# Row maxima of a windowed attention: spread over the partitions through DRAM in GpSimd's queue instead of by TensorE transposes, exponentials one quarter later

## The chip, the cores and the metric

The kernel runs on one core of a Trainium2 chip. The metric is the time of one execution on the device, in microseconds (us), as the median of repeated runs. The times of the kernel before are 628.92, 630.24 and 630.98 us (median 630.24).

## The reference

One layer of a diffusion backbone, in float32, on 1024 latent tokens of width 1024 (a grid of 16 rows by 64 columns) and 256 context tokens. Cut to what matters here:

```python
h  = rmsnorm(x, norm_g) * (1 + scale) + shift          # adaLN from c
q, k, v, za, u, bg, cg, zc = split(h @ w_in)           # eight blocks of 512 columns
q, k = rmsnorm per head of 64                          # 8 heads
s_lat = rope(q) . rope(k) * scale + bias               # each query sees an 8 x 16 window
s_ctx = q . kc * scale                                 # and all 256 context keys
p = softmax(concat(s_lat, s_ctx))                      # one softmax over both
o = p_lat @ v + p_ctx @ vc
attn = o * silu(za)
conv = bg * conv3(cg * u) * silu(zc)
out = x + gate * (concat(attn, conv) @ w_out)
```

The softmax needs, for every query, a maximum over its keys. The kernel holds scores with keys on the partitions and queries along the free dimension, so that maximum runs across partitions, and the result has to stand on all 128 partitions to be subtracted.

## The kernel before, in words

**Stages.** Up to about 60 us the kernel loads and transposes x and multiplies the first columns; from there to about 273 us it projects q, k, v for the eight heads and spills them to DRAM; from about 274 to 512 us it runs the attention; then it ends the convolution and multiplies by `w_out`. Float32 products are split into high and low float32r parts, three TensorE matmuls for each product (`mm3`).

**The attention stage** is a loop over quarters (`quarter(n)`): a head has four quarters of 256 queries, so there are 32 with scores and a few more at the end that drain the pipeline. TensorE's idle places are filled with projection work for the gates and the convolution: the generator `fill`, one step of which (a *tick*) is six matmuls of 512 columns into the tile `pu`. The table `TICKS` says how many ticks each quarter gets; its length is the number of quarters.

**One quarter** issues on TensorE the latent scores (tile `pss`), the context scores of the next quarter (`pc`), the transposes of row maxima (`pmx`), ticks, and the products with v of an earlier quarter (tile `po`: `lat_out` for the window, `ctx_out` for the context keys of two quarters at once, in every second quarter and at its very start; such a quarter is called early in the code). VectorE adds the bias (`sb<-pss,bt`), takes maxima (`mx<-pc,sc`, `mx<-mx,sb`), subtracts them (`sc<-sc,mg`, `sb<-sb,mg`) and makes the low parts (`plc`, `pll`) of what ScalarE exponentiated (`phc`, `phl`).

**The maxima** (`maxima(e)`, L1135 on). `mx` holds for each partition and query the maximum over the keys of that partition. TensorE transposes up to two blocks of 128 queries of it (`pmx<-ci,mx`), VectorE reduces along the free dimension to `rm` (queries on the partitions, one column for each block). The inner function `back` then transposes a broadcast of `rm` on TensorE (`pmx<-ci,rm`), which puts each maximum on all partitions, and ScalarE copies it from PSUM to `mg`. `back` is called between the matmuls of `ctx_out` or `ctx_scores`, so that TensorE has other work while VectorE reduces.

**Order.** In this stage every instruction of TensorE, ScalarE and VectorE, and GpSimd's computing instructions, are chained in the order in which the code issues them. The DMAs of SyncE and GpSimd are not; the scheduler places them in their queues, and a queue then runs in order. Quarter n exponentiates the scores of quarter `e = n - 2` and multiplies with v those of `o = n - 3`.

Of the kernel before, what the change touches and what calls it, by code (L numbers as in the profile page):

```python
# [10 lines left out]
F32 = mybir.dt.float32  # L11
# [8 lines left out]
P = 128  # L20
# [6 lines left out]
NH, HD = 8, 64  # L27
# [2 lines left out]
CTXT = 3  # L30
FORDER = [4, 5, 6, 0, 1, 2, 3, 7]

TICKS = [2, 3, 3, 3, 3, 2, 3, 3, 2] + 2 * (8 * [3] + 2 * [4]) + 3 * [3] + [5, 4, 4]
EPS = 1e-6


# [3 lines left out]
def body(tc, es, x, ctxt, w_ada, b_ada, w_in, q_g, k_g, rpbr, w_out, vecs, cst, out):  # L40
    nc = tc.nc
# [20 lines left out]
    pe, act, dve, pool = every = [ordered(e) for e in (nc.tensor, nc.scalar, nc.vector, nc.gpsimd)]  # L62
# [27 lines left out]
    def many(name, n, shape):  # L90
        return [dr.tile(shape, F32, name=f"{name}{i}")[:] for i in range(n)]
# [14 lines left out]
    v_d = many("v_d", NPAIR, [P, 2, 2, NB + 2, HD + 1])  # L106
    kc_d = many("kc_d", NPAIR, [P, 2, L])
    ri_d = many("ri_d", NPAIR, [2, T])


    cp = es.enter_context(sbuf("cp"))
    ci = cp.tile([P, P + 2], F32, name="ci")
    ident = ci[:, 0:P]
# [213 lines left out]
    def do_frees(most):  # L327
        while most > 0 and slow and slow[0][2] is not None and not slow[0][0]:
            slow.pop(0)[1]()
            most -= 1  # L330
        return most
# [508 lines left out]
    for m in range(1, 4):  # L840
        k, new, last = 2 * m, m < 3, m == 3
# [169 lines left out]
    class head:  # L1011
# [31 lines left out]
        def ctx_scores(self, g, between=None):  # L1043
            pc = psm.tile([P, 2, 256], F32, name="pc", tag="C", bufs=2)
            q = self.q[:, 1, g * 256:(g + 1) * 256]
            for i in range(2):
                if i and between:
                    between()
                for l in range(2):
                    pe.matmul(pc[:, i], self.kc[:, l, i * P:(i + 1) * P], q,  # L1050
                              start=(i == 0 and l == 0), stop=(i == 1 and l == 1), skip_group_check=True)
            sc = ap.tile([P, 2, 256], F32, name="sc", tag="sc", bufs=4)
            act.copy(sc, pc)
            self.cps[g] = sc, pc

# [58 lines left out]
    def pair_of(n):  # L1114

        h, g = divmod(n, 4)
        return [(a, heads[h], 2 * g + a) for a in range(2)] if 0 <= h < NH else []
# [12 lines left out]
    def turned(n):  # L1130

        g = n % 4
        return [b for b, there in (((2 * g + 2) % NB, n + 1 < 4 * NH), (2 * g + 1, n >= 0)) if there][::-1 if g < 3 else 1]

    def maxima(e):  # L1135

        blocks = turned(e) if e < 4 * NH else []
        nb = len(blocks)
        if not blocks:
            return None  # L1140
        pm = psm.tile([P, 512], F32, name="pmx", tag="C", bufs=2)
        for i, b in enumerate(blocks):
            pe.transpose(pm[:, i * P:(i + 1) * P], mx[:, b * P:(b + 1) * P], ident)
        rm = ap.tile([P, 2], F32, name="rm", tag="rm", bufs=8)
        dve.tensor_reduce(rm[:, :nb], pm[:, :nb * P].rearrange("p (i k) -> p i k", i=nb), AX.X, ALU.max)

        def back():
            for i in range(nb):
                pe.transpose(pm[:, 256 + i * P:256 + (i + 1) * P], rm[:, i:i + 1].broadcast_to([P, P]), ident)
            v, step = mg[:, blocks[0] * P:], (blocks[-1] - blocks[0]) * P or P  # L1150
            act.copy(bass.AP(v.tensor, v.offset, [list(v.ap)[0], [step, nb], [1, P]]),
                     pm[:, 256:256 + nb * P].rearrange("p (i k) -> p i k", i=nb))
        return back

    def quarter(n):

        live = lambda m: 0 <= m < 4 * NH  # L1160
        ticks = TICKS[n]
        e, o = n - 2, n - 3
        left = do_frees(1) + 2 if n > 2 else 3
        back = maxima(e) if e >= 0 else None
        while lat_rest:
            lat_rest.pop()()
        early = live(o) and o % 2
        if early:
            heads[o // 4].ctx_out(o % 4, back)
        do_dves(left)  # L1170
        if gating and next(gating[0], "end"):
            gating.pop(0)
        now = pair_of(n)
        for i, hd_, j in now:
            hd_.scores(j, sbank[:, i])
        if n == 0:
            next(fill)
            ticks -= 1
        ctx_now = [m for m in ([0, 1] if n == 0 else [n + 1]) if live(m)]
        for m in ctx_now:  # L1180
            heads[m // 4].ctx_scores(m % 4, back if n >= 2 and not early else None)
        if back and not early and not ctx_now:
            if not now:
                next(fill, None)
                ticks -= 1
            back()
        def biased():
            sb = sbs[n] = sb_new()
            bt = now[0][1].bt[:].rearrange("p v n -> p (v n)")[:, :1128].rearrange("p (a n) -> p a n", a=2)
            for at, slot, w_ in (((0, 31, 8), (8, 15, 16)), ((0, 0, 31),), ((0, 0, 31),), ((0, 0, 15), (15, 39, 8)))[n % 4]:  # L1190
                dve.tensor_tensor(sb[:, :, at * 12:(at + w_) * 12], sbank[:, :, at * 12:(at + w_) * 12],
                                  bt[:, :, slot * 12:(slot + w_) * 12], ALU.add)

        if now and not (early or n < 2):
            biased()
        if live(e):
            ctx_rest = heads[e // 4].ctx_exp(e % 4)
            sb = sbs.pop(e)
            w = both(sb, e)
            w4 = w.rearrange("p a (c r) -> p a c r", r=12)  # L1200
            dve.tensor_tensor(w4, w4, maxima_of(e), ALU.subtract)
            exps[e] = [ap.tile([P, 2, 384], F32R, name=m, tag=m, bufs=b) for m, b in (("phl", 2), ("pll", 1))]
            ph, pl = (both(v, e) for v in exps[e])
            act.activation(ph, w, AF.Exp)
            act.activation(w, w, AF.Exp)
        for _ in range(n > 0):
            next(fill, None)
        done = []
        if o >= 0:
            pho, plo = exps.pop(o)  # L1210
            for i, hd_, j in pair_of(o):
                hd_.lat_out(j, pho[:, i], plo[:, i])
                if j in (5, 7):
                    done.append((hd_, j // 7))
                    if j == 7 and hd_.s:
                        ready.append(hd_.p)
        if now:
            if early or n < 2:
                biased()
            for m in ctx_now:  # L1220
                heads[m // 4].ctx_max(m % 4)
            for i, hd_, j in now:
                hd_.lat_max(j, sbs[n][:, i])
        back = maxima(-1) if n == 1 else None
        if live(e):
            ctx_rest()
            lat_rest.append(lambda: dve.tensor_tensor(pl, w, ph.bitcast(F32), ALU.subtract))
            if n + 1 >= len(TICKS) or TICKS[n + 1] == 2:
                lat_rest.pop()()
        for _ in range(ticks - (n > 0)):  # L1230
            next(fill, None)
        if back:
            back()
        for hd_, bank_ in done:
            hd_.finish(bank_)
        do_acts()

    heads = [head(h) for h in range(NH)]
# [13 lines left out]
    fill = fillers()  # L1252
# [20 lines left out]
    for n in range(NT + 3):  # L1273


        p, t = divmod(n, NB)
# [51 lines left out]
        if 1 < n <= NT + 1:  # L1328
            m, r = n - 2, (n - 2) % NB
# [69 lines left out]
    with sbuf("att") as ap, psum("psb") as psb:  # L1399
        sbank = psb.tile([P, 2, 512], F32, name="pss")  # L1400
        strict[:] = every
        mx = ap.tile([P, T], F32, name="mx")
        sb_new = lambda: ap.tile([P, 2, 384], F32, name="sb", tag="sb", bufs=3)
        mg = ap.tile([P, T], F32, name="mg")
        heads[0].load_v()
        for n in range(len(TICKS)):
            h, g = divmod(n, 4)
            if 0 < h < NH and g == 0:
                heads[h].load_v()
            if h + 1 < NH and g:  # L1410
                nx = heads[h + 1]
                for load in ((nx.masks, nx.load_q), (nx.load_k,), ())[g - 1]:
                    load()
            quarter(n)
            if ready:
                p = ready.pop()
                if p < NPAIR - 1:
                    gating.append(gated(p))
                else:
                    recip(p, ap)  # L1420
        for step in gating:
            for _ in step:
                do_acts()
                do_dves()
        for _ in fill:
            do_dves()
            do_acts()
        while soon or slow:
            do_dves()
            do_acts()  # L1430
        strict[:] = []
# [80 lines left out]
    for n, (nh, t) in enumerate([(0, 6), (0, 7)] + [(1, t) for t in range(NB)]):  # L1512
        pieces = [slice(0, 384), slice(384, 512)] if (nh, t) == (1, NB - 1) else [slice(0, 512)]
# [33 lines left out]


# [18 lines left out]
```

## Time and profile before

| | before |
|---|---|
| median of three timed runs | 630.24 us (628.92 to 630.98) |
| span of the profiled execution | 629.7 us |
| TensorE (PE) busy | 621.4 us, 99% |
| VectorE (DVE) busy | 433.5 us, 69% |
| ScalarE (ACT) busy | 325.5 us, 52% |
| GpSimd (POOL) busy | 78.0 us, 12% |
| granted TensorE clock | 1.000 of full speed |

The page gives the profiled execution by its span alone, 629.7 us from the first instruction to the last; no other time of that execution is on it, and the span lies inside the three timed runs. Busy time on PE is modelled from pipelined matmuls, so a slot of a matmul is better read from the distance between two starts than from a duration. "L55" is a wrapper through which most engines are called, so groups are told apart by the names of the tiles.

### The profile page before, as it was taken

What the parts mean: (1) busy time and instruction counts of PE and PEld (TensorE: products, weight loads), DVE (VectorE), ACT (ScalarE), POOL (GpSimd) and SP (SyncE); (2) the same over time, 40 slices, a digit from 0 to 9 for tenths busy, and PEclk for the clock granted to TensorE, in tenths of its full rate; (3) what the DMA queues carried; (4) which work ended last, traced back from release to release, by engine and by line L of the source; (5) the groups of instructions that cost most, each with busy time, mean ns of one, the idle gap of its engine ahead of it and who ended that gap; (6) DMA issues with size and microseconds to landing.
All of it is one profiled execution on the core that took longest, in us unless ns stands there. A gap on an engine that the chain in (4) does not pass through costs nothing.

```text
span 629.7 us, 9816 instructions
## 1 busy us (share of the span) xinstructions
PE 621.4 (99%) x3391; PEld 530.9 (84%) x3392; DVE 433.5 (69%) x889; ACT 325.5 (52%) x712; POOL 78.0 (12%) x102
## 2 busy tenths in 40 slices
PE   8999999999999999999999999999999999999998
PEld 3577899999999999888888888888878788878887
DVE  1887858866867855478897888987998755495111
ACT  4777835424625545346576568567774844451000
POOL 1305014123123222100000000000000002004200
PEclk9999999999999999999999999999999999999999
DMA  8983738967784994886566472857441235973631
GB/s 318 346 288 119 187 97 275 280 200 242 250 272 149 303 321 167 312 258 221 151 213 179 153 236 70 267 199 256 125 136 61 73 95 160 338 230 117 218 101 51
DMA packets 104030, 126.45 MB, mean 201 GB/s; under 512 B 10689, under 2 KB 70553, under 8 KB 102700
## 3 DMA queue, kind: packets, MB, share of 16 engines
q1 hardware_dynamic: 97516, 114.24, 55.3%
q10 hardware_dynamic: 6208, 11.05, 5.7%
q0 software_dynamic: 256, 0.54, 0.3%
q8 instruction: 27, 0.44, 0.3%
q14 instruction: 23, 0.19, 0.1%
HBM read 89.04 MB, written 39.04 MB: 203 GB/s over the span
## 4 chain that ended last, share of the span: by engine, by line
PE 88%; DMA 5%; ACT 3%; DVE 2%; issue 1%; ACTq 1%; SPq 1%; DVEq 0%
PE pu L55 25%; PE pacc L55 21%; PE po L55 8%; PE acc L55 6%; PE pout L76 4%; PE pout L74 4%; PE pout L75 4%; PE tr L55 4%; PE cacc L55 4%; PE pss L55 3%; DMA woraw<-in_w_out 2%; PE pc L55 2%; PE pmx L55 2%; DMA xx<-in_x 2%; DMA xr<-in_x 1%; PE trA L55 1%
## 5 line engine op out<-in xcount | busy, mean ns | idle before, releaser
L55 PE MATMUL pu<-h,uh 128*128 128x512 f32 x544 | 169.9, 394 | 0.3 <-ACT zs L55 0.3
L55 PE MATMUL pacc<-w,h 128*128 128x384 f32 x768 | 138.4, 337 | 0.0
L55 PEld LDWEIGHTS pacc<-w,h 128*128 128x128 f32 x768 | 132.7, 188 | 0.2
L55 PEld LDWEIGHTS pu<-h,uh 128*128 128x128 f32 x544 | 97.7, 188 | 17.4 <-ACT zs L55 0.6
L55 PE MATMUL pu<-h,ul 128*128 128x512 f32 x272 | 106.6, 392 | 0.0
L55 PEld LDWEIGHTS pu<-h,ul 128*128 128x128 f32 x272 | 51.1, 188 | 11.2
L55 POOL TENSOR_TENSOR ss<-ss,few 128x4 f32<-128x4 f32 (+1 forms) x40 | 41.9, 1049 | 124.8 <-DVE ss L55 124.8
L74 PE MATMUL pout<-woh,yh 128*128 128x512 f32 (+2 forms) x136 | 51.7, 380 | 1.0 <-ACT yh L1471 1.0
L75 PE MATMUL pout<-wol,yh 128*128 128x512 f32 (+2 forms) x136 | 51.6, 380 | 0.0
L76 PE MATMUL pout<-woh,yl 128*128 128x512 f32 (+2 forms) x136 | 50.9, 380 | 0.0
L55 PE MATMUL acc<-h,w 128*128 128x512 f32 x144 | 38.1, 405 | 0.8 <-ACT h L55 0.8
L55 ACT ACTIVATE sq<-pacc 128x256 f32<-128x256 f32 x32 | 12.4, 387 | 47.7 <-PE pacc L55 47.2
L55 ACT ACTIVATE phc<-sc 128x512 fp32r<-128x512 f32 x32 | 20.3, 634 | 30.1 <-DVE sc L55 30.1
L55 DVE TENSOR_REDUCE rm<-pmx 128x2 f32<-128x256 f32 (+1 forms) x33 | 13.7, 416 | 29.8 <-PE pmx L55 29.4
L55 DVE TENSOR_TENSOR mx<-mx,sb 128x372 f32<-128x372 f32 (+2 forms) x64 | 31.9, 498 | 1.9
L55 ACT COPY mg<-pmx 128x256 f32<-128x256 f32 (+1 forms) x33 | 12.0, 365 | 39.1 <-PE pmx L55 33.9
L55 PE MATMUL po<-phl,v 128*65 128x276 f32 (+2 forms) x192 | 32.0, 269 | 0.0
L55 DVE TENSOR_REDUCE ss<-sq 128x4 f32<-128x260 f32 (+1 forms) x40 | 15.6, 391 | 23.7 <-ACT sq L55 23.6
L55 ACT ACTIVATE qn<-pacc,ss 128x64 f32<-128x64 f32 x128 | 30.1, 332 | 3.0 <-POOL ss L55 3.0
L55 PEld LDWEIGHTS acc<-h,w 128*128 128x128 f32 x144 | 25.5, 188 | 6.5 <-ACT h L55 1.2
L74 PEld LDWEIGHTS pout<-woh,yh 128*128 128x128 f32 x136 | 25.6, 188 | 6.1 <-ACT yh L1471 1.5
L76 PEld LDWEIGHTS pout<-woh,yl 128*128 128x128 f32 x136 | 25.6, 188 | 5.1 <-DVE yl L1472 0.4
(159 smaller groups left out, 1158.7 us busy)
## 6 DMA issues: line engine op xcount, KB each, us to landing
uraw<-in_w_in SPq DMA_DIRECT2D x34, 256.0 KB
q_d<-qs SPq DMA_DIRECT2D x32, 256.0 KB
k_s<-k_d SPq DMA_DIRECT2D x8, 1024.0 KB
q_s<-q_d SPq DMA_DIRECT2D x16, 512.0 KB
wr<-in_w_in SPq DMA_DIRECT2D x40, 192.0 KB
slab<-in_w_ada SPq DMA_DIRECT2D x6, 1024.0 KB
v_d<-vs SPq DMA_DIRECT2D x20, 260.0 KB
v<-v_d SPq DMA_DIRECT2D x16, 325.0 KB
```

The lines of the kernel that those rows point to most:

```text
L55: i = emit(*a, **kw)
L74: i = pe.matmul(ps, ah, bh, start=first, stop=False)
L75: pe.matmul(ps, ah, bl, start=False, stop=False)
L76: pe.matmul(ps, al, bh, start=False, stop=last)
```

## The change

Five edits belong together:

- `maxima` no longer returns `back`. After the reduction to `rm`, GpSimd's queue stores `rm` to a scratch tensor `m_d[e]` in DRAM (128 partitions, one or two single elements from each), and then loads it from there into `mg` with a read that repeats the row for all 128 partitions (256 columns in one DMA where the two blocks are neighbours, otherwise two DMAs of 128). The 64 transposes `pmx<-ci,rm` and the 33 copies `mg<-pmx` on ScalarE are gone.
- Quarter n exponentiates `e = n - 3` instead of `n - 2`, and multiplies `o = n - 4`. `maxima(n - 2)` now stands behind the scores, no longer at the start of the quarter.
- `TICKS` has 36 entries instead of 35, and 113 ticks instead of 110; fewer ticks are left for after the attention.
- `sc` has five buffers instead of four, `sb` four instead of three.
- GpSimd's scratch for DMA descriptors is set to 8192 bytes.

```diff
-TICKS = [2, 3, 3, 3, 3, 2, 3, 3, 2] + 2 * (8 * [3] + 2 * [4]) + 3 * [3] + [5, 4, 4]
+TICKS = [2, 3, 3, 4, 3, 2, 3, 3, 2] + 2 * (8 * [3] + 2 * [4]) + 3 * [3] + [4, 4, 4, 3]
...
+    m_d = many("m_d", 4 * NH + 1, [2, P])
...
-            sc = ap.tile([P, 2, 256], F32, name="sc", tag="sc", bufs=4)
+            sc = ap.tile([P, 2, 256], F32, name="sc", tag="sc", bufs=5)
...
         dve.tensor_reduce(rm[:, :nb], pm[:, :nb * P].rearrange("p (i k) -> p i k", i=nb), AX.X, ALU.max)
-
-        def back():
-            for i in range(nb):
-                pe.transpose(pm[:, 256 + i * P:256 + (i + 1) * P], rm[:, i:i + 1].broadcast_to([P, P]), ident)
-            v, step = mg[:, blocks[0] * P:], (blocks[-1] - blocks[0]) * P or P
-            act.copy(bass.AP(v.tensor, v.offset, [list(v.ap)[0], [step, nb], [1, P]]),
-                     pm[:, 256:256 + nb * P].rearrange("p (i k) -> p i k", i=nb))
-        return back
+        pool.dma_start(m_d[e][0:nb].rearrange("i k -> k i"), rm[:, :nb])
+        if nb == 2 and blocks[1] == blocks[0] + 1:
+            pieces = [(blocks[0], m_d[e])]
+        else:
+            pieces = [(b, m_d[e][i:i + 1]) for i, b in enumerate(blocks)]
+        for b, rows in pieces:
+            n = rows.shape[0] * P
+            pool.dma_start(mg[:, b * P:b * P + n], bass.AP(rows.tensor, rows.offset, [[0, P], [1, n]]))
...
-        e, o = n - 2, n - 3
+        e, o = n - 3, n - 4
         left = do_frees(1) + 2 if n > 2 else 3
-        back = maxima(e) if e >= 0 else None
...
-            heads[o // 4].ctx_out(o % 4, back)
+            heads[o // 4].ctx_out(o % 4, None)
...
-            heads[m // 4].ctx_scores(m % 4, back if n >= 2 and not early else None)
-        if back and not early and not ctx_now:
-            if not now:
-                next(fill, None)
-                ticks -= 1
-            back()
+            heads[m // 4].ctx_scores(m % 4)
...
         if now and not (early or n < 2):
             biased()
+        if n >= 2:
+            maxima(n - 2)
         if live(e):
...
-        sb_new = lambda: ap.tile([P, 2, 384], F32, name="sb", tag="sb", bufs=3)
+        sb_new = lambda: ap.tile([P, 2, 384], F32, name="sb", tag="sb", bufs=4)
...
-    nc = bacc.Bacc("TRN2", target_bir_lowering=False, num_devices=1)
+    nc = bacc.Bacc("TRN2", target_bir_lowering=False, num_devices=1, dynamic_dma_scratch_size=8192)
```

**TensorE, the fifth quarter (n = 4).** Before, it starts with the transposes of `mx`; in this kernel it is an early quarter, so the context products `po<-phc` and `po<-plc` of the first head follow, with the transposes of `rm` between them:

```order
L55 MATMUL pmx<-ci,mx 128x128 [waits DVE_49,Activation_49]
L55 MATMUL pmx<-ci,mx 128x128
L55 MATMUL po<-phc,v_3314 65x512 [waits Activation_49]
L55 MATMUL po<-phc,v_3314 65x512
L55 MATMUL po<-plc,v_3314 65x512 [waits DVE_49]
L55 MATMUL po<-phc,v_3314 65x512
L55 MATMUL pmx<-ci,rm 128x128 [waits DVE_49]
L55 MATMUL pmx<-ci,rm 128x128
L55 MATMUL po<-phc,v_3314 65x512
L55 MATMUL po<-plc,v_3314 65x512
L55 MATMUL pss<-q_s,k_s 128x288 [waits DMAHW2_49,DMAHW0_49]
```

In the changed kernel the same quarter reads:

```order
L55 MATMUL pss<-q_s,k_s 128x288 [waits DMAHW2_49,DMAHW0_49,DVE_49]
L55 MATMUL pss<-q_s,k_s 128x288 x3
L55 MATMUL pc<-q_s,kc_s 128x256 [waits DVE_49]
L55 MATMUL pc<-q_s,kc_s 128x256 x3
L55 MATMUL pmx<-ci,mx 128x128 [waits DVE_49,Activation_49]
L55 MATMUL pmx<-ci,mx 128x128
L55 MATMUL pu<-h_257,uh 128x512 x2
```

The transposes of `rm` are gone, those of `mx` stand behind the scores, and the context products have moved to the next quarter.

**GpSimd's queue in quarters 11 to 13.** `m_d_117` is the scratch of `maxima(8)`, `m_d_118` that of `maxima(9)`, and so on. In the changed kernel:

```order
L1147 DMA m_d_117<-rm 128x2x1 [waits DMASW4_49,DVE_49]
L1154 DMA mg<-m_d_117 128x256 [waits DMASW4_49]
L1147 DMA m_d_118<-rm 128x2x1 [waits DMASW6_49,DVE_49]
L1147 DMA m_d_119<-rm 128x2x1 [waits DVE_49]
L1154 DMA mg<-m_d_118 128x256 [waits DMASW6_49,DMASW0_49]
L1154 DMA mg<-m_d_119 128x256 [waits DMASW7_49]
```

Everywhere else a store is followed by its own load; here the load of `maxima(9)` stands behind the store of `maxima(10)`, which waits for VectorE's next reduction.

**VectorE in quarter 12 of the changed kernel**, where the scores of quarter 9 are exponentiated. `rm` here is the reduction of `maxima(10)`; `sc<-sc,mg` waits for the load of `m_d_118` (DMASW0):

```order
L55 TENSOR_TENSOR pll<-sb,phl 128x2x288 [waits PE_49,Activation_49]
L55 TENSOR_TENSOR sb<-pss,bt 128x2x96 [waits DMAHW1_49,DVE_49,PE_49]
L55 TENSOR_TENSOR sb<-pss,bt 128x2x192
L55 TENSOR_REDUCE rm<-pmx 128x2 [waits PE_49]
L55 TENSOR_TENSOR sc<-sc,mg 128x512 [waits DMASW0_49]
L55 TENSOR_TENSOR sb<-sb,mg 128x2x372
L55 TENSOR_TENSOR mx<-pc,sc 128x256 [waits Activation_49]
L55 TENSOR_TENSOR mx<-mx,sb 128x24x12 [waits DVE_49] x2
L55 TENSOR_TENSOR plc<-sc,phc 128x2x256 [waits Activation_49]
```

The reduction has moved from the start of VectorE's quarter to just ahead of the subtraction, and the subtraction waits for a DMA instead of for ScalarE's copy.

More of the change, by code (lines that the diff above doesn't have):

```diff
@@ L1139, in maxima @@
         if not blocks:
-            return None
+            return
         pm = psm.tile([P, 512], F32, name="pmx", tag="C", bufs=2)
@@ L1223, in quarter @@
                 hd_.lat_max(j, sbs[n][:, i])
-        back = maxima(-1) if n == 1 else None
+        if n == 1:
+            maxima(-1)
         if live(e):
@@ L1231, in quarter @@
             next(fill, None)
-        if back:
-            back()
         for hd_, bank_ in done:
```

## The prediction

> **What bounds the kernel now.** I read the page first: which engine is busy, and whether the TensorE clock holds.
>
> ```profile
> PE 621.4 (99%) x3391; PEld 530.9 (84%) x3392; DVE 433.5 (69%) x889; ACT 325.5 (52%) x712; POOL 78.0 (12%) x102
> PEclk9999999999999999999999999999999999999999
> ```
>
> TensorE is busy nearly all of the span, at a clock that does not drop. The change touches the attention stage, so next the busy times by stretch, for the whole stage and for its middle:
>
> ```profile
> 274.00:512.00 238.00, 236.81 (x1338) 198.80 (x1337) 198.62 (x355) 153.11 (x260) 0.26 (x4) 1.00 0.51 165
> 340.00:500.00 160.00, 158.92 (x899) 133.41 (x898) 139.05 (x250) 107.08 (x178) 0.26 (x4) 1.00 0.51 162
> ```
>
> After the width of the stretch come PE, PEld, DVE, ACT and POOL. TensorE stands still for 1.2 of 238 us. VectorE is second, with 139.05 of 160 us, and the DMA engines are busy for 0.51 of the time. Then the groups of VectorE's middle stretch, and what it waited for in the stage:
>
> ```profile
> L55 DVE TENSOR_REDUCE rm<-pmx 128x2 f32<-128x256 f32 x22 | 9.3, 424 | 17.5 <-PE pmx L55 17.2
> L55 DVE TENSOR_TENSOR sc<-sc,mg 128x512 f32<-128x512 f32 x21 | 14.4, 683 | 0.9 <-ACT mg L55 0.8
> L55 DVE TENSOR_TENSOR sb<-sb,mg 128x744 f32<-128x744 f32 (+2 forms) x21 | 17.6, 837 | 0.0
> L55 DVE TENSOR_TENSOR plc<-sc,phc 128x512 fp32r<-128x512 f32 x21 | 14.4, 684 | 0.0
> L55 DVE TENSOR_TENSOR mx<-mx,sb 128x372 f32<-128x372 f32 (+2 forms) x42 | 20.8, 495 | 1.2
> L55 DVE TENSOR_TENSOR mx<-pc,sc 128x256 f32<-128x256 f32 x20 | 8.3, 415 | 0.0
> ...
> DVE rm L55 <- PE pmx L55: 29.4, 23, 4.1
> ```
>
> There are 22 reductions in 160 us, so a quarter lasts 160 / 22 = 7.27 us and holds 139.05 / 22 = 6.3 us of VectorE's work. VectorE idles about 1 us a quarter, almost always because it is early and waits for TensorE's transposes. So TensorE's list of matmuls sets the pace and VectorE follows closely: what leaves TensorE is gained, as long as nothing makes VectorE lose more than that 1 us.
>
> **What the change removes.** The slot of two transposes is read from the distance of starts, with and without them between the context scores, in two quarters:
>
> ```profile
> 340.02 0.40 PE L55 MATMUL pc<-q_s,kc_s 128*128 128x256 f32 x2
> 340.25 0.38 PE L55 MATMUL pmx<-ci,rm 128*128 128x128 f32 x2
> 340.39 0.48 PE L55 MATMUL pc<-q_s,kc_s 128*128 128x256 f32 x2
> 340.71 0.63 PE L55 MATMUL pu<-h,uh 128*128 128x512 f32 x2
> ...
> 347.95 0.64 PE L55 MATMUL pc<-q_s,kc_s 128*128 128x256 f32 x4
> 348.42 0.63 PE L55 MATMUL pu<-h,uh 128*128 128x512 f32 x2
> ...
> L55 PE MATMUL pmx<-ci,rm x64: 269/272/324, 277.2 to 510.1; 128*128 128x128 f32 x64
> ...
> L55 ACT COPY mg<-pmx 128x256 f32<-128x256 f32 (+1 forms) x33 | 12.0, 365 | 39.1 <-PE pmx L55 33.9
> ```
>
> With the pair, four `pc` matmuls take 340.71 - 340.02 = 0.69 us; without, 348.42 - 347.95 = 0.47. A pair costs 0.22 us, one transpose 0.11 (the 272 ns of its row is a modelled, overlapping duration). 64 of them are **7.0 us** of a saturated engine. The 33 copies on ScalarE, 12.0 us, lie beside TensorE on an engine that waits 33.9 us for those very transposes; I take 0 for them. The stage's pace becomes 7.27 - 0.22 = 7.05 us.
>
> Costed at nothing as well: the 36th quarter (no matmuls are added, `fill` has a fixed number of ticks, and three ticks move from behind the attention into it); the larger buffers; the smaller descriptor scratch (one store and one or two loads are under way in a quarter). What hides the three moved ticks is the matmuls left behind the stage; without them the end could move by up to 1 us either way.
>
> **What it adds: a round trip through DRAM.** From the end of VectorE's reduction to `mg`, before its subtraction a quarter later. The trace has GpSimd DMAs only at the end, where the reciprocals take the same way:
>
> ```profile
> 521.23 0.77 POOL L526 DMA_DIRECT2D ri<-rs_d  x1 [57.99 <-DMA rs_d<-ob]
> 524.22 0.55 POOL L528 DMA_DIRECT2D ri_d<-ri  x1 [2.21 <-DVE ri L55]
> 526.45 2.07 POOL L532 DMA_DIRECT2D rb<-ri_d  x4 [1.68 <-DMA ri_d<-ri]
> ...
> 523.66 0.25 DVE L55 RECIPROCAL ri<-ri 128x16 f32<-128x16 f32 x1 [5.90 <-DMA ri<-rs_d]
> 523.83 1.22 DVE L55 TENSOR_TENSOR ul<-uraw,uh 128x512 fp32r<-128x512 f32 x2
> 524.97 3.05 DVE L55 SCALAR_TENSOR_TENSOR cv<-cu,vecT,cv 128x512 f32<-128x512 f32 x4
> ...
> rb<-ri_d POOLq DMA_DIRECT2D x4, 128.0 KB, 6.5
> ri<-rs_d POOLq DMA_DIRECT2D x1, 8.0 KB, 2.4
> ...
> DMA to landing us min/median/max: 5.1/6.5/7.8
> ```
>
> The reciprocal ends at 523.91, its store is issued at 524.22 (0.31 later), and the dependent load at 526.45 (2.23 after that). A load lands 2.4 us after its issue when small (`ri`, 8 KB), and 5.1 to 7.8 us when it spreads 128 KB over the partitions like `mg`'s (`rb`, four issued back to back, so that 5.1 is the one least held up by its fellows). So the round trip R is 0.31 + 2.23 + 2.4 = 4.9 us at best, 7.6 with 5.1. `mg`'s loads have the size of `rb`'s, but mostly come alone; I take the middle, a landing of 4 us, R = 6.5.
>
> What is there to hide it? The subtraction stands right behind the next reduction in VectorE's order, so one round of VectorE's work, 6.3 us, lies between. If R is longer, VectorE waits; but then the next reduction follows its subtraction by 6.3 us, so two quarters take R + 6.3, and VectorE's pace is (R + 6.3) / 2. That passes TensorE's 7.05 only at R = 7.8. With 6.5 it is 6.4: hidden. Behind the waiting subtraction stand VectorE's maxima, `plc` and `pll`; for them TensorE waits with `ctx_out` at the start of every second quarter. For quarters of two ticks, and those with two loads of `mg` (one more issue, 0.5 us from the `rb` row, 2.07 / 4), I add 0.5 us in all (0 to 2).
>
> One place is not hidden: in GpSimd's queue the load of `maxima(9)` stands behind the store of `maxima(10)`, so it is issued only after the reduction that directly precedes the subtraction needing it. VectorE then waits 0.31, 0.55 for the store's issue (the `ri_d` row) and the landing: 0.9 + 4 = 4.9 us (3.3 to 6.0). From there to the end of `plc` its work is 0.68 + 0.84 + 0.42 + 2 x 0.50 + 0.68 = 3.6 us, so `plc` stands 8.5 us after the reduction. TensorE meanwhile has three ticks, one `lat_out` and the first of `ctx_out`:
>
> ```profile
> 348.42 0.63 PE L55 MATMUL pu<-h,uh 128*128 128x512 f32 x2
> 349.12 0.63 PE L55 MATMUL pu<-h,uh 128*128 128x512 f32 x2
> ...
> 342.10 0.43 PE L55 MATMUL po<-phl,v 128*65 128x288 f32 x2
> 342.89 0.39 PE L55 MATMUL pu<-h,uh 128*128 128x512 f32 x1
> ...
> 345.75 0.70 PE L55 MATMUL po<-phc,v 128*65 128x512 f32 x2
> 346.28 0.39 PE L55 MATMUL po<-plc,v 128*65 128x512 f32 x1
> ```
>
> Three matmuls take 0.70, a tick 1.4; `lat_out` of a first quarter 0.79; `plc` is due 0.53 into `ctx_out`. Together 4.2 + 0.8 + 0.5 = 5.5 us after the transposes, and the reduction ends some 0.6 after them, so `plc` is due 4.9 us after it. TensorE stands still for 8.5 - 4.9 = 3.6, taken as **3.5 us** (2.0 to 4.7).
>
> **The sum.** The span, 629.7 us, lies 0.5 below the median, 630.2, so a difference worked out in the span is put on the median: 630.2 - 7.0 + 3.5 + 0.5 = **627.2 us**. If the waits ahead of `pmx` go too, up to 1.2 us more (TensorE's whole idle time in the stage).
>
> **A rule that speaks against it.** VectorE's two-input work runs while GpSimd issues: the four `rb` issues took 2.07 us, 0.52 each, beside 3.05 us of convolution taps without a gap. The Trainium skill, SBUF — State Buffer, section "SBUF: two separate sides", warns that GpSimd cannot write DMA descriptors while VectorE runs a copy, cast or scalar operation in a mode that takes their shared port pair. Its section "Who interferes with whom" leaves out tensor_tensor and reductions, which make up this stage. If the trap sprang here, each of the two issues would wait for at most one VectorE instruction, 0.84 us by the `sb<-sb,mg` row: R = 6.5 + 1.7 = 8.2, pace 7.25, and 29 quarters x 0.2 = 6 us, so 633. The trace shows no such stretching of an issue; I give it 0.03, within the first rival.
>
> **The rivals.**
>
> *The round trip is too long, and VectorE becomes the bound* (slower). It decides at R = 7.8, a landing of 5.3 us. For it: `rb`'s median is 6.5, the DMA engines are busy half the time with the next head's loads, the store writes single elements. Against it: four `rb` loads stood in one another's way. With 6.5, R = 9.0, pace 7.65, 0.6 x 29 quarters = 17.4, and the late load costs 0.9 + 6.5 + 3.6 - 4.9 = 6.1: 630.2 - 7.0 + 17.4 + 6.1 = 647. Just past the threshold, R = 8.7, it is 630.2 - 7.0 + 13 + 6 = 642. The Trainium skill, DMA: Bandwidth & Descriptors, section "Latency and other measured facts", has DRAM's access at 0.2 us on average and 2 us under high load; an estimate from that page, 1.8 us more on both ways, makes R 4.9 + 3.6 = 8.5 and the time about 639. Chance 0.28.
>
> *The gain is eaten* (no change): landings near 5.1, R = 7.6. The pace still holds, the late load costs 4.7, short quarters their 2: 630.2 - 7.0 + 6.7 = 629.9. Chance 0.17.
>
> *All is hidden*, the late load at its least and the waits gone: 630.2 - 7.0 + 2.0 - 1.2 = 624. It belongs to faster.
>
> That the change doesn't do what it says is excluded: the instructions in their order show the 64 transposes gone and no matmul added.
>
> **How the numbers follow.** About 0.3% (1.9 us) is what a measurement of this kernel can tell from no change. Forecast with its better variant, faster: 0.55. Within 0.3%: 0.17. Slower: 0.28. The forecast's own range is 623 to 628.3. The range given goes down to 623 and up to 640, which takes in the gain eaten and half of the slower case; about 0.15 is left above and 0.04 below.
>
> **What would show it right or wrong.** `pmx<-ci,rm` and `mg<-pmx` are gone; the distance of reductions in full quarters is 7.0 to 7.1 us; POOL has 33 stores and 40 loads, with loads landing in 3 to 5 us; VectorE waits for `mg<-m_d` once for about 5 us (quarter 12), otherwise below 1; TensorE waits once, 2 to 5 us, for `plc`. Wrong, if VectorE's waits for `mg<-m_d` exceed 1 us in most quarters, with loads landing 5.3 us or more after issue, and TensorE waits for VectorE in each of them.

## The result, and the profile after

The changed kernel takes 819.49 us (median of four runs, 809.93 to 823.73) where the kernel before, run beside it, takes 629.88 (628.92 to 630.98): a ratio of 1.297 with a 95% interval of 1.289 to 1.304. The ratio is worked out from the fast runs alone, without the one of 823.73 us; by the two medians it is 1.301. The forecast was 627.2 us, the range 623 to 640. Both were wrong, by far.

The page of the changed kernel, its busy times and the granted clock:

```profile
PE 662.5 (81%) x3328; PEld 550.2 (67%) x3328; DVE 434.9 (53%) x889; ACT 316.2 (39%) x679; POOL 123.2 (15%) x175
PEclk9999999999999978878768788788779789899999
```

The span is 817.7 us. TensorE is idle for 817.7 - 662.5 = 155 us, against 8 before; and although it has 64 matmuls fewer, it is busy for 662.5 - 621.4 = 41 us longer, and its clock falls to six to eight tenths in most of the slices in which it keeps stopping. 147 us more of standing still and 41 us more of busy time for fewer matmuls are the whole difference of the two spans, 188 us.

The same middle stretch of the attention stage as before the change, by windows (width, then PE, PEld, DVE, ACT, POOL, clock, DMA share, GB/s), and VectorE's groups in it:

```profile
340.00:500.00 160.00, 104.46 (x486) 82.11 (x485) 76.58 (x136) 54.42 (x88) 17.03 (x29) 0.80 0.55 112
```

```profile
L55 DVE TENSOR_TENSOR sc<-sc,mg 128x512 f32<-128x512 f32 x12 | 8.3, 689 | 64.6 <-DMA mg<-m_d 64.6
L55 DVE TENSOR_REDUCE rm<-pmx 128x2 f32<-128x256 f32 x12 | 5.0, 419 | 14.7 <-PE pmx L55 14.7
```

A matmul of this stretch takes on average 104.46 / 486 = 0.215 us at a clock of 0.80, where it took 158.92 / 899 = 0.177 at 1.00. Twelve reductions now fit where there were 22, and VectorE stands 64.6 of the 160 us in front of the subtraction. What the engines waited for, from 270 to 720 us (total, times, longest), and the landing of the stores and loads (count, size, median):

```profile
POOL mg L1154 <- DMA m_d<-rm: 311.1, 33, 12.2
ACT phc L55 <- DVE sc L55: 215.3, 29, 20.7
DVE sc L55 <- DMA mg<-m_d: 176.6, 26, 19.9
...
PE po L55 <- ACT phc L55: 74.4, 14, 11.5
...
PE pu L55 <- ACT zs L55: 26.5, 3, 13.5
```

```profile
mg<-m_d POOLq DMA_DIRECT2D x24, 128.0 KB, 5.4
mg<-m_d POOLq DMA_DIRECT2D x16, 64.0 KB, 3.8
m_d<-rm POOLq DMA_DIRECT2D x31, 1.0 KB, 10.2
```

The waits form a chain. GpSimd waits 311.1 / 33 = 9.4 us for each store before it can issue the load; VectorE waits for the load; ScalarE's exponentials wait for VectorE; TensorE waits for the exponentials. Three quarters on GpSimd's timeline (start, duration, idle time before and its releaser):

```profile
342.36 0.72 POOL L1147 DMA_DIRECT2D m_d<-rm  x1 [0.54 <-DVE rm L55]
353.45 0.57 POOL L1154 DMA_DIRECT2D mg<-m_d  x1 [10.37 <-DMA m_d<-rm]
354.01 0.72 POOL L1147 DMA_DIRECT2D m_d<-rm  x1
366.97 0.56 POOL L1154 DMA_DIRECT2D mg<-m_d  x1 [12.24 <-DMA m_d<-rm]
372.44 0.72 POOL L1147 DMA_DIRECT2D m_d<-rm  x1 [4.90 <-DVE rm L55]
383.91 1.10 POOL L1154 DMA_DIRECT2D mg<-m_d  x2 [10.76 <-DMA m_d<-rm]
```

From a store's issue to its load's issue 11.1, 13.0 and 11.5 us pass, where the prediction had 2.23. The store at 354.01 follows the load of the round before without a gap: the reduction was ready, but the queue was not.

### The profile page after: what moved, and what is told of

Read it like the earlier page. It is cut to its first block, busy times and chain, and to the rows that moved or that the text cites. A ratio compares the mean times of both kernels' runs of the same rounds, so it can differ in the third digit from the quotient of the medians.

```text
span 817.7 us, 9775 instructions
## 1 busy us (share of the span) xinstructions
PE 662.5 (81%) x3328; PEld 550.2 (67%) x3328; DVE 434.9 (53%) x889; ACT 316.2 (39%) x679; POOL 123.2 (15%) x175
## 4 chain that ended last, share of the span: by engine, by line
PE 45%; DMA 23%; issue 22%; DVE 3%; POOL 2%; ACT 2%; SPq 0%; ACTq 0%; POOLq 0%; DVEq 0%
DMA m_d<-rm 16%; PE pacc L55 16%; PE acc L55 5%; DMA mg<-m_d 4%; PE pu L55 4%; PE pout L76 4%; PE pout L74 4%; PE pout L75 4%; PE tr L55 3%; PE cacc L55 3%; POOL mg L1154 1%; PE po L55 1%; DMA q_d<-qs 1%; DMA xx<-in_x 1%; POOL m_d L1147 1%
## 5 line engine op out<-in xcount | busy, mean ns | idle before, releaser
L55 PE MATMUL pu<-h,uh 128*128 128x512 f32 x544 | 184.2, 422 | 26.5 <-ACT zs L55 26.5
L55 PEld LDWEIGHTS pu<-h,uh 128*128 128x128 f32 x544 | 104.9, 204 | 46.2 <-ACT zs L55 27.8
L55 DVE TENSOR_TENSOR sc<-sc,mg 128x512 f32<-128x512 f32 x32 | 22.1, 690 | 176.6 <-DMA mg<-m_d 176.6
L55 PE MATMUL po<-phc,v 128*65 128x512 f32 x64 | 29.7, 558 | 74.4 <-ACT phc L55 74.4
L1154 POOL DMA_DIRECT2D mg<-m_d x40 | 22.3, 558 | 311.1 <-DMA m_d<-rm 311.1
L55 PEld LDWEIGHTS po<-phc,v 128*65 128x65 f32 x64 | 10.8, 191 | 84.0 <-ACT phc L55 80.3
L55 PEld LDWEIGHTS pu<-h,ul 128*128 128x128 f32 x272 | 54.4, 200 | 12.9 <-DVE ul L55 0.2
L55 PE MATMUL pss<-q_s,k_s 128*128 128x372 f32 (+2 forms) x128 | 31.6, 380 | 13.7 <-DVE sb L55 13.7
L55 ACT COPY sc<-pc 128x512 f32<-128x512 f32 x32 | 18.7, 587 | 61.0 <-PE pc L55 55.0
L55 PEld LDWEIGHTS pss<-q_s,k_s 128*128 128x128 f32 x128 | 27.1, 241 | 20.9 <-DVE sb L55 16.6
L1147 POOL DMA_DIRECT2D m_d<-rm x33 | 23.7, 717 | 85.5 <-DVE rm L55 83.5
```

The source lines that it names most:

```text
L55: i = emit(*a, **kw)
L1147: pool.dma_start(m_d[e][0:nb].rearrange("i k -> k i"), rm[:, :nb])
L1154: pool.dma_start(mg[:, b * P:b * P + n], bass.AP(rows.tensor, rows.offset, [[0, P], [1, n]]))
```

## The experiments

Two theories stood at the start: A, the *store* is slow; B, the *load* is slow (the prediction's own rival). Kernels whose maxima are constant leave the real ones out; they say so in their expectations. In all full kernels from `e1` on that load `mg` by DMA, GpSimd's DMAs are chained in the order of the code, so the load that stood behind the next store (`m_d_118`) no longer does.

**m1: the store by itself.** A small kernel stores the same kinds of elements in different layouts, each store followed at once by a load of what it wrote.

> A kernel that copies x to the output and, ahead of that, stores small tiles to DRAM from GpSimd's queue and then from SyncE's, nothing else running; each store is followed in the same queue by a load of its first element, so the time from a store's issue to the load's issue is the store's landing. Cases, four times each: a2 = 256 single elements into 1 KB (the change's store), b1 = 128 single elements into 512 bytes, c16 = 128 runs of 64 bytes, d64 and e512 = 256 single elements 64 or 512 bytes apart, f1 = one partition's 1 KB, h8 = 128 runs of 8 bytes, g128 = 8 runs of 128 bytes. Theory A (the many tiny writes to DRAM make the store slow): a2 about 10 us, b1 and h8 about 6 to 8, c16, f1, g128 about 2; d64 and e512 about 10 if their number counts, about 2 to 3 if their lying in one short stretch of DRAM counts; SyncE's queue the same. Theory B (the bulk transfers beside it make any small store slow): all cases 1.7 to 2.6 us here.

GpSimd's packed store of two single elements from each partition (`pa`) and of one (`pb`), and 64-byte runs (`pc`):

```profile
50.80 0.76 POOL L33 DMA_DIRECT2D pa<-src  x1
59.57 0.51 POOL L33 DMA_DIRECT2D b_pa<-pa  x1 [8.01 <-DMA pa<-src]
60.08 0.57 POOL L33 DMA_DIRECT2D pb<-src  x1
68.41 0.51 POOL L33 DMA_DIRECT2D b_pb<-pb  x1 [7.75 <-DMA pb<-src]
...
103.05 0.57 POOL L33 DMA_DIRECT2D pc<-src  x1
105.03 0.51 POOL L33 DMA_DIRECT2D b_pc<-pc  x1 [1.42 <-DMA pc<-src]
```

Issue to issue is 8.8 to 15.5 us for the kernel's store, 8.3 to 15.5 for half as many elements, 2.0 to 2.4 for runs of 64 bytes. The first three of the kernel's stores ran beside the copy of x, and SyncE's own series of the same cases ran beside all of them, so the long ones may hold a share of that. SyncE's last two packed stores of 256 elements took 8.3 and 8.4 us. That does not yet clear GpSimd's queue: beside one of GpSimd's packed stores, SyncE's store of 64-byte runs took 6.7 us as well (issued at 93.90, its load at 100.55), and 1.4 twice later on. But the same 256 single elements from GpSimd's queue, written 64 bytes apart, took 2.25 us: it is neither their number nor the queue by itself. Only packing them into one short stretch of DRAM is dear. Two of the expected prices were off: 128 runs of 8 bytes took 3.4 to 3.6 us instead of 6 to 8, and one partition's 1 KB took 4.0 twice and then 1.8.

**m2: the same beside other transfers.**

> The same cases from GpSimd's queue, beside a chain of 512 KB loads on SyncE's queue, each waiting for the one before. Theory A: a2 10 to 12 us, c16, f1 and g128 2.5 to 4. Theory B: all cases about 10 us.

Beside SyncE's bulk loads the packed store took 10.4 to 13.8 us, the spread one 2.7 to 2.9, one contiguous row 2.3 to 3.2. The changed kernel's own stores, 7.9 to 13.0 us from a store's issue to its load's and 10.4 on average, are like the first of these. The packed stores hold up the other queue too: from 55 to 91 us, with GpSimd's stores of 128 packed elements under way, the DMA engines moved 59 GB/s, and 160 GB/s from 105 to 131 us beside the spread ones, with the same chain of bulk loads.

**e1: nobody waits for the store.**

```diff
-            pool.dma_start(mg[...], bass.AP(rows.tensor, rows.offset, [[0, P], [1, n]]))
+            in_turn(pool.dma_start(mg[...], bass.AP(m_c.tensor, m_c.offset, [[0, P], [1, n]])))
```

> The changed kernel with its stores, but mg is loaded from a row of DRAM written once at the start, so no load waits for a store; each load stands right behind its quarter's store in GpSimd's queue. It leaves out the row maxima from the exponentials (one constant is subtracted for all queries and the exponent halved, so that sums stay finite). If the wait for the store is the whole loss (theories A and B): VectorE's waits for mg fall from 177 us to under 15, the clock returns to 1.0, and the time is 624 to 630 us. If the loads alone, or the schedule with 36 quarters, are at fault: above 650 us.

735.05 us, ratio 1.168 (1.161 to 1.175). The expectation failed: GpSimd's waits for the store are gone, yet the time is 105 us over the kernel before. The landing of `mg`'s loads in this kernel:

```profile
DMA to landing us min/median/max: 7.6/10.3/16.8
mg<-m_c POOLq DMA_DIRECT2D x24, 128.0 KB, 12.1
m_d<-rm POOLq DMA_DIRECT2D x31, 1.0 KB, 11.5
```

In the changed kernel the median was 4.3 us. By these medians a load of 128 KB issued right behind the packed store, though independent of it, lands about when the store does (0.7 us after the store's issue, and 12.1 from there, against 11.5). So the store costs twice: whoever waits for it, and what is queued behind it.

**e2: the same data, stored as rows.** VectorE first transposes `rm` in 32 x 32 blocks, so that the 256 maxima leave as 8 runs of 128 bytes; all else, the real round trip included, is kept.

```diff
-        pool.dma_start(m_d[e][0:nb].rearrange("i k -> k i"), rm[:, :nb])
+        dve.transpose(rt[:, :32 * nb], rm[:, :32 * nb])
+        in_turn(pool.dma_start(m_d[e][0:nb].rearrange("i (b k) -> b i k", b=4), ...))
```

> The changed kernel with the store's shape changed: VectorE turns the reduced maxima in blocks of 32 x 32, so that each store is 8 runs of 128 bytes from 4 partitions (4 for one block) instead of 256 single elements; each load is also kept ahead of the next store in GpSimd's queue. Theory A: GpSimd waits about 2 us for each store instead of 9.4, VectorE's waits for mg fall below 20 us, and the time is 624 to 632 us (VectorE has about 0.2 us more per quarter). Theory B: the store still lands after 7 to 12 us and the time stays at 790 to 820 us.

681.13 us, ratio 1.079 (1.074 to 1.084). Stores land in 3.5 us, loads in 3.4:

```profile
m_d<-rt POOLq DMA_DIRECT2D x31, 1.0 KB, 3.5
DMA to landing us min/median/max: 3.1/3.4/7.9
```

The layout of 33 stores of 1 KB, with the loads in the order of the code, was worth 138 of the 190 us. But some 50 us are left that neither theory had.

**m3: how close is too close, and what is held up.**

> A measurement of its own, all in GpSimd's queue and without the kernel. 128 single elements, one from each partition, are stored 4, 8, 16, 32, 64 or 256 bytes apart, each store followed by a load of one element of what it wrote; then one lone element. After that a load of one row to all 128 partitions (128 KB), issued with nothing before it, right behind a packed store of 256 elements, or right behind the same elements 64 bytes apart. If what costs is the number of writes that fall into one stretch of 64 bytes (16 of them took 8.3 us, 8 of them 3.5), store issue to load issue halves with the spacing: about 8.3, 4.5, 2.7, 2.3, 2.2, 2.2 us. If it is a fixed price of anything closer than 64 bytes, the first four are equal, 8 us. The row's load lands 3.5 to 4.5 us after its issue when alone. If a packed store also holds up what is queued behind it on the same DMA engines, it lands 10 us or more after its issue behind the packed store and 4 to 5 behind the spread one; if only the waiting for the store's own end is dear, all three land alike.

128 single elements 4, 8, 16 and 64 bytes apart, then a 128 KB load issued behind a packed and behind a spread store:

```profile
39.62 0.57 POOL L33 DMA_DIRECT2D p4b<-src  x1
47.48 0.51 POOL L33 DMA_DIRECT2D b_p4b<-p4b  x1 [7.29 <-DMA p4b<-src]
47.98 0.57 POOL L33 DMA_DIRECT2D p8b<-src  x1
51.71 0.51 POOL L33 DMA_DIRECT2D b_p8b<-p8b  x1 [3.16 <-DMA p8b<-src]
...
64.47 0.57 POOL L33 DMA_DIRECT2D p16b<-src  x1
66.78 0.51 POOL L33 DMA_DIRECT2D b_p16b<-p16b  x1 [1.74 <-DMA p16b<-src]
...
85.42 0.57 POOL L33 DMA_DIRECT2D p64b<-src  x1
87.44 0.51 POOL L33 DMA_DIRECT2D b_p64b<-p64b  x1 [1.45 <-DMA p64b<-src]
...
133.21 0.57 POOL L62 DMA_DIRECT2D pack<-m_c  x1
141.36 0.53 POOL L33 DMA_DIRECT2D z_pack<-pack  x1 [7.58 <-DMA pack<-m_c]
...
171.52 0.66 POOL L62 DMA_DIRECT2D apart<-m_c  x1
175.47 0.53 POOL L33 DMA_DIRECT2D z_apart<-apart  x1 [3.30 <-DMA apart<-m_c]
```

Issue to issue is 7.9 to 12.3 us at 4 bytes (7.9 for the one shown, when SyncE's queue had nothing left to issue), 3.5 to 3.7 at 8, 2.0 to 2.3 at 16 and no less at 32, 64 and 256 (up to 2.4); a lone element takes 1.8 to 2.0. So the price grows with how closely the writes lie, but only above four of them to 64 bytes; it does not halve all the way. (64 bytes is a unit chosen for counting: no run shows how long the stretch is within which writes get in one another's way.) The load behind the packed store needs 8.0 to 8.7 us, where I expected 10 or more, behind the spread one 3.9 to 4.3, with no store 3.5 to 4.2: theory A's second half, apart from the kernel. The Trainium skill, DMA: Bandwidth & Descriptors, section "Queues, rings and completion order", has a rule that fits this, given there for the queues of SyncE and ScalarE: a DMA's semaphore increment is a strongly ordered write, landing only after every earlier write of its DMA engine, across that engine's queues. No run looked inside the engines, so that this is the reason is not shown.

**e3: the schedule alone** (TensorE's transposes kept, no DMA added).

> The change without its transport: 36 quarters, exponentials a quarter later, the deeper buffers, the maxima behind the scores, but the maxima are spread by TensorE's transposes and ScalarE's copies as before; no DMA is added. If the new order costs nothing by itself, 627 to 633 us. If part of the 51 us that were left with row-wise stores comes from the order (TensorE waits there for ScalarE's zs behind late exponentials), 640 to 680 us.

648.71 us, ratio 1.030 (1.028 to 1.032): the order that I had costed at nothing costs 19 us without any transport. One place in it, on PE, ACT and PEld:

```profile
381.25 0.39 PE L55 MATMUL pu<-h,ul 128*128 128x512 f32 x1
...
381.67 0.82 ACT L55 ACTIVATE sb<-sb 128x744 f32<-128x744 f32 x1
...
382.76 1.28 ACT L55 ACT_TABLE_LOAD   x1
384.05 1.09 ACT L55 ACTIVATE zs<-pu 128x512 f32<-128x512 f32 x2
...
384.70 0.72 PE L55 MATMUL pu<-h,uh 128*128 128x512 f32 x2 [3.06 <-ACT zs L55]
...
388.72 1.26 PE L55 MATMUL pss<-q_s,k_s 128*128 128x372 f32 x4
```

A gate unit ended with the tick at 381.25. The next tick needs a tile `pu` that ScalarE's silus must read first, and these stand behind the exponentials and a table load. TensorE stands still for 3.06 us, and then runs four `pss` matmuls in 1.26 us that took 0.67 at 369.63.

**e4, e5: the transport without the store, and with a spread store.** Both against `e1`: in `e4` the line of the store is gone; in `e5` the same single elements are written 64 bytes apart:

```diff
-    m_d = many("m_d", 4 * NH + 1, [2, P])
+    m_d = many("m_d", 4 * NH + 1, [P, 2, 16])
...
-        in_turn(pool.dma_start(m_d[e][0:nb].rearrange("i k -> k i"), rm[:, :nb]))
+        in_turn(pool.dma_start(m_d[e][:, 0:nb, 0], rm[:, :nb]))
```

> The loads alone: as in the kernel with constant maxima, but the stores of rm are left out altogether (the maxima are a constant 195 and the exponent is halved, so the softmax is computed with other numbers). 33 of GpSimd's DMAs go, and each load waits only for its target to be free. If the packed store was what held up the loads behind it, they land in 3 to 5 us and the time is 624 to 640 us. If loads of this size cost that much by themselves beside the kernel's other transfers, they still land around 10 us and the time stays near 735.

> One edit against the kernel with constant maxima that took 735 us: the store of rm is there, of the same elements at the same places in the queue, but they are written 64 bytes apart instead of packed (nobody reads them; the loads take the constant row). If packing is the cause, the loads land in 4 to 5 us and the time is 625 to 645 us. If a store of 256 single elements as such holds up what stands behind it, it stays at 720 to 740 us.

649.54 us (ratio 1.032, 1.030 to 1.033) and 651.54 (1.034, 1.033 to 1.036). The landing of `mg`'s loads in `e5`:

```profile
DMA to landing us min/median/max: 3.2/4.5/8.7
```

Against `e1` one address pattern was changed, and 83.5 us went with it. By the medians the spread store costs 2.0 us (`e5` less `e4`); but TensorE stands still for 5.8 us at the start of the stage in `e4` and not in `e5`, so elsewhere the store may cost up to some 8. Both times lie 7 to 10 us above the upper end of what I expected; the schedule, which takes 648.7 us in `e3` beside them, would account for that.

**e6, e7, e8: one tick of the tick table moved.** The fourth entry of `TICKS` back to 3, in `e3`, `e4` and `e2`; the 33rd goes from 4 back to 5, so that the sum stays 113.

```diff
-TICKS = [2, 3, 3, 4, 3, 2, 3, 3, 2] + 2 * (8 * [3] + 2 * [4]) + 3 * [3] + [4, 4, 4, 3]
+TICKS = [2, 3, 3, 3, 3, 2, 3, 3, 2] + 2 * (8 * [3] + 2 * [4]) + 3 * [3] + [5, 4, 4, 3]
```

> The schedule alone (TensorE's transposes kept), with the tick table as it was for the first 31 quarters: the fourth entry is 3 instead of 4, the 36 entries still sum to 113. Theory: the 19 us of the schedule alone come from that one tick more. It moves every later tick one place, so that the gate units end one tick before the end of a quarter; ScalarE's silus, issued at the end of the quarter, then release the tile pu too late for the last tick, and TensorE stands still. With 3 the next tick stands behind the scores of the next quarter, as before: 629 to 635 us. Rival: the exponentials a quarter later hold ScalarE up by themselves, and it stays at 645 to 650.

> The loads alone, without stores (maxima constant, exponent halved), with the fourth entry of the tick table at 3. This is the change with a transport that nobody waits for. If the transposes were worth their 7 us, and the table accounts for the rest, 623 to 632 us (the kernel that it is compared with had one more wait of 5.8 us at the start of the stage, which may stay). If the transposes were worth nothing, 632 to 640; if the table isn't the cause, 648.

> The whole change with row-wise stores (8 runs of 128 bytes, VectorE transposing rm first), which took 681 us, with the fourth entry of the tick table at 3. If the tick table's cost and the round trip's waits add up, 660 to 668 us; if the waits for pu were hidden behind waits for the loads, 672 to 681.

640.71 us, 636.74 and 666.86: 8.0, 12.8 and 14.3 us less than their partners. TensorE's waits in `e6`:

```profile
PE pmx L55 <- DVE rm L55: 6.4, 7, 1.5
PE pu L55 <- ACT zs L55: 1.2, 1, 1.2
```

The wait for the silus is down to 1.2 us (7.1 in `e3`), as the theory had it. The profiled span falls by 12.4 us (649.4 to 637.0), 6.5 of it less standing still and 5.9 less busy time for the same 3391 matmuls (628.1 to 622.2). But 11 us of the schedule's cost stay by the medians, 7.3 by the profiled spans. The wait for `rm`, 6.4 here and in `e3`, is one that my test kernels made by keeping the transposes where TensorE now arrives too early; the changed kernel does not have it. `e7` does without it, and is 7.5 us above the kernel before, with one standstill of 6.0 us at the start of the stage, where VectorE's bias waits for `q_d` and with it `pss`. The kernels with stores have less than 1 us of it there (0.9 in the changed kernel, 0.3 in `e8`). `e6` and `e7` lie some 5 us above what the theory gave, and `e7` falls where transposes worth nothing would put it, which `e9` below speaks against; the rest of the schedule's price is not settled. `e8` came out as expected.

`e8` less `e7` is what a dependent round trip costs even with row-wise stores (33 block transposes on VectorE among it): 30 us, and some 6 more if the standstill that `e7` has and `e8` has not is set aside. Two pairs of its GpSimd timeline:

```profile
299.62 0.60 POOL L1157 DMA_DIRECT2D m_d<-rt  x1 [4.99 <-DVE rt L55]
301.58 0.56 POOL L1165 DMA_DIRECT2D mg<-m_d  x1 [1.36 <-DMA m_d<-rt]
...
388.40 0.60 POOL L1157 DMA_DIRECT2D m_d<-rt  x1 [4.32 <-DVE rt L55]
394.49 0.56 POOL L1165 DMA_DIRECT2D mg<-m_d  x1 [5.49 <-DMA m_d<-rt]
```

From store to load it is 2.5 us or less in 11 of the 33, and 3.9 to 7.8 in 13; VectorE waits for `mg` ten times, 30.7 us in all. A round trip that fits on the average does not fit in its worst quarters, and what was lost there was not won back here.

**e9: what the change removes.** The kernel before without the 64 transposes.

```diff
-                pe.transpose(pm[:, 256 + i * P:256 + (i + 1) * P], rm[:, i:i + 1].broadcast_to([P, P]), ident)
...
+            act.copy(other[:, :nb * P], pm[:, :nb * P])
```

> The kernel before, without its 64 transposes of rm, all else kept: ScalarE's copies read the transposed mx instead and go to a tile that nobody reads, the maxima are a constant 195 and the exponent is halved. This prices what the change removes. If a pair is worth its slot of 0.22 us on a saturated TensorE, 622 to 624 us; if VectorE takes over at once, or the transposes stood in gaps, 628 to 631.

625.18 us, ratio 0.993 (0.991 to 0.995): a gain of 4.1 us between the medians (5.7 between the profiled spans, 629.7 and 624.0), between the two theories and nearer to the first. TensorE's standing still in the stage grows at once:

```profile
274.00:512.00 238.00, 235.18 (x1301) 195.66 (x1300) 202.03 (x361) 156.95 (x265) 0.27 (x4) 1.00 0.52 168
```

It is idle for 2.8 us of the 238, against 1.2. About 4 us, then, was to be won from these transposes in the old order of work, with their replacement wholly hidden.

## Why the prediction was wrong

- **What bounds the kernel** was read rightly: TensorE, with VectorE close behind. `e9` shows that the transposes were on the path.
- **The gain, 7.0 us**, measured 4.1 by the medians of `e9`. Of the rest 1.6 us came back as idle time of TensorE in the stage; 1.3 us are not accounted for.
- **The store, 2.23 us: the step that failed.** The price was taken from the `ri_d` row, 8 KB in 128 runs of 64 bytes. The kernel's store is 1 KB in 256 single elements, packed into 1 KB. "The nearest row" was nearest by queue and direction, not by the form of what is written. In the changed kernel 7.9 to 13.0 us passed from issue to issue, 10.4 on average, and written as rows the store landed in 3.5. `e1` and `e5` show a second cost that no term of the sum held: the loads queued behind a packed store land late. The single elements were named in the first rival, in passing, and given no price.
- **The load, 4 us**, was near: 4.3 median over all 40 loads of the changed kernel, but 5.4 over the 24 of 128 KB that the 4 us was worked out for, and 3.8 over the 16 of 64 KB. The rival that ended on the right side hung its price on a long load, and so ended at 642 to 647.
- **The threshold, R = 7.8 us**, was the right question. With a median landing of 10.2 and 4.3, R is 0.31 + 10.2 + 4.3 = about 15, and (15 + 6.3) / 2 = 10.6 us a quarter. The 33 stores from 276.2 to 688.8 us make 412.6 / 32 = 12.9. The formula left out that GpSimd's queue is serial: 0.72 for the store, 9.4 of waiting and 0.56 for the load are 10.7 us a quarter on GpSimd alone, so its queue, not only VectorE's order, came near to the limit; and it left out TensorE's clock. What makes 12.9 out of 10.7 was not taken apart.
- **The schedule at nothing** was wrong by 19 us (`e3`; 6.4 of them are the wait for `rm` that the test kernel made), of which the fourth entry of the tick table is 8 (`e6`), or 13 with the transposes gone (`e7`). I counted the ticks and not where they fall: one tick more in the fourth quarter puts the end of each gate unit one tick ahead of the place where ScalarE's silus are issued. The shorter waits for the silus in `e6` bear this out; what is left of the schedule's price is open.
- **The late load, 3.5 us**, was not measured by itself. In the changed kernel it is there (store at 396.35, next store at 405.23, its load at 408.87), as one of many waits.
- **The trap of GpSimd's descriptors** (0.03) did not spring: a store's issue takes 0.72 us and a load's 0.56 beside VectorE's work, by the rows of GpSimd's timeline, and the store's issue takes 0.76 in `m1` too, where VectorE stands idle.
- **The smaller descriptor scratch** was never undone by itself; m1 to m3, which kept the default size, show the slow store as well.

In sums: 629.4 before; 649.5 with the new schedule and a transport that nobody waits for; 651.5 with a spread store; 681.1 with a real round trip by rows; 735.1 with the packed store, nobody waiting; 819.5 as changed. No version that computes the maxima beat the kernel before.

## What to carry to other kernels

Price a small DMA by a row with the same *form of writes*: the number of runs, their length, and how closely they lie. A column of single elements that becomes a row in DRAM should be turned on the chip first, or spread. And where a table sets the order, "no instruction added" is not "no cost": look at which engine's release each moved group now waits for.

## What the runs showed of the hardware

- 128 or 256 writes of 4 bytes packed into 512 bytes or 1 KB of DRAM take 7.9 to 15.5 us from issue to the issue of a dependent load (`m1`, `m3`); 128 of them 8 bytes apart 3.5 to 3.7; 16 or more apart 2.0 to 2.4.
- An independent load behind such a store lands about 4 us later than behind a spread one (8.0 to 8.7 against 3.9 to 4.3 us in `m3`), and another queue is slowed too (59 against 160 GB/s in `m2`).
- TensorE paid this standstill twice. After the 3.06 us in `e3` its clock by windows was 0.57, and then full again:

```profile
386.00:390.00 4.00, 4.00 (x14) 2.82 (x13) 0.00 (x0) 0.18 (x1) 0.00 (x0) 0.57 0.00 0
390.00:394.00 4.00, 4.00 (x30) 3.55 (x30) 3.25 (x6) 3.45 (x5) 0.00 (x0) 1.00 0.00 0
```

The Trainium skill, TensorE: Matmul & The Clock Gate, section "What's actually happening", has half rate after an idle window of about 3.4 us; the trace agrees nearly: TensorE's idle time was a little shorter, by an end that is modelled.
